# Feed-forward units in pairs by Strassen's seven products, in a two-layer decoder step on one core

## The chip, the core and the metric

One NeuronCore of a Trainium2 chip runs the whole program. The metric is the device time of one execution in microseconds (us), lower is better. Engines are named as in the profile: PE (TensorE, matmuls), PEld (its weight loads), DVE (VectorE), ACT (ScalarE), POOL (GpSimd), SP (SyncE, which issues most transfers).

## What is computed

A decoder trunk of two layers over 520 tokens (512 of a prompt, 8 of a sample group), model width 1024. Layer 0 mixes with retention and a spatial gating unit, layer 1 with a convolution module. After each mixer comes the feed-forward, which the change is about:

```python
x = x + y
f = rmsnorm(x, norm_ffn_g[l]) @ ffn_w1[l]          # 1024 -> 4096
x = x + jnp.square(jax.nn.relu(f)) @ ffn_w2[l]     # 4096 -> 1024
...
rmsnorm: x * rsqrt(mean(x * x) + 1e-6) * g
```

All data are float32.

## The kernel before

Activations lie in SBUF with features on the 128 partitions, in eight chunks `c` of 128 features by T = 520 tokens; tokens are taken in two halves of HALF = 260. A matmul takes a 128x128 piece of a weight (stationary) and 128x260 of activations (moving) and adds into a bank of PSUM. To keep float32 accuracy each operand is split into a high part in the type fp32r and the rest: ACT writes the high part (line 120 for weights), DVE subtracts it from the source (line 121, a tensor operation that reads two tiles in SBUF). Each product is made as high x high, high x low and low x high.

A "unit" (`unit`, `unit_mm`) makes 128 output features of all 520 tokens from 1024 input features. `load_w` fetches its weights (128 x 8 x 128, 512 KB, one transfer on SP's queue, three buffers `raw`), `split_half` splits four of the eight pieces at a time (five buffers each of `wh` and `wl`), and 8 x 3 x 2 = 48 matmuls follow, line 137. 

The feed-forward `ffn` takes the 4096 hidden features in four blocks `blk`. For a block, eight up units make 1024 hidden features: the result in PSUM is multiplied by the row of 1/rms `nm.r` and cut at zero by DVE (`ft`, line 671), squared and split by ACT (`fh`, line 673), POOL (`ff`, line 675) and DVE (`fl`, line 676). Then eight down units add the block's share to `x` (line 691). `Norm` holds `x * g` in split form (`hi`, `lo`), before the factor 1/rms; `finish` makes the row of 1/rms and is called in the middle of the first up unit. In the last block of layer 1, the last unit is made half by half and followed by the final norm and the output (`last_half`).

The other stages use the same helpers: projections of layer 0 (`in_units`), retention, the output projection (`opr` for the retention rows, `ops` for the gating rows), and in layer 1 `conv_in`, the taps (DVE, and ACT with POOL: line 798; some on PE by the diagonal tiles `diag`, line 726), and `conv_out`. A block between `ops` and the first feed-forward prepares the sample tokens' convolution from rows kept before (`hist`, line 703, on POOL).

Tiles come from pools. Each tag has a number of buffers, and an instruction that writes a tile waits for the last reader of the one that had the buffer. `big` has five buffers of 128 x 8 x 520; `mp` holds what the mixers need for the whole program; PSUM has two double banks `mm` and four single ones `auxA`, `auxB`. The order of the instructions on each engine is made ahead by a planner, from the program's order as priority and its own estimates of times. Each engine then runs its instructions strictly in that order.

Of the kernel before, what the change touches and what calls it, by code (L numbers as in the profile page):

```python
# [71 lines left out]
def trunk_kernel(tc, a, o):  # L72
    nc = tc.nc
    te, ve, se, pe_ = nc.tensor, nc.vector, nc.scalar, nc.gpsimd
    with ExitStack() as st:
# [4 lines left out]
        mp = st.enter_context(tc.tile_pool(name="mp", bufs=2))  # L80
        ps = st.enter_context(tc.tile_pool(name="ps", bufs=2, space=PSUM))
        dr = st.enter_context(tc.tile_pool(name="dr", bufs=1, space=DRAM))

# [25 lines left out]
        def load_w(ap, row, col):  # L109
            raw = wp.tile([P, C, P], F32, name="raw", tag="raw", bufs=3)  # L110
            nc.sync.dma_start(raw, ap[row:row + D, col:col + P].rearrange("(k p) n -> p k n", p=P))
            return raw
# [3 lines left out]
        def split_half(src, i):  # L116
            hi = wp.tile([P, KH, P], F32R, name="wh", tag="wh", bufs=5)
            lo = wp.tile([P, KH, P], F32R, name="wl", tag="wl", bufs=5)
            sp = src[:, i * KH:(i + 1) * KH, :]
            se.activation(hi, sp, AF.Copy)  # L120
            ve.tensor_sub(lo, sp, hi.bitcast(F32))  # L121
            return hi, lo

# [6 lines left out]
        def unit_mm(pts, w, x, mid=None):  # L130
            """pts (two halves of the tokens) = w^T x, three products of the split parts."""
            xh, xl = x
            for k in range(C):
                hi, lo = w[k // KH]
                for i, (wt, xt) in enumerate(((hi, xh), (hi, xl), (lo, xh))):
                    for hf in range(2):
                        te.matmul(pts[hf], wt[:, k % KH, :], xt[:, k, hf * HALF:(hf + 1) * HALF],  # L137
                                  start=k == 0 and i == 0, stop=k == C - 1 and i == 2)
                if mid and k == 4:
                    mid()  # L140

        def unit(pt, ap, row, col, x, mid=None):
            """pt = ap[row:row+1024, col:col+128]^T x."""
            unit_mm(halves(pt), split_w(load_w(ap, row, col)), x, mid=mid)
# [61 lines left out]
        def rsqrt_row(pts, e_col, eps, out, nxt=None):  # L206
            """out = (pts + eps) ** -0.5: ScalarE's estimate and one Newton step."""
# [16 lines left out]
        def row_mean(src, name):  # L224
            """mean over features of [P, T] partial sums, on every partition (two psum tiles)."""
# [7 lines left out]
        class Norm:  # L233
            """x * g split in two parts, and the row of 1/rms, chunk by chunk."""

            def __init__(self, g, name, final=False):
                self.g, self.name = g, name
                self.hi = None if final else bigt(name + "h", F32R)
                self.lo = None if final else bigt(name + "l", F32R)
                self.acc = tmp(name + "acc")  # L240
                self.y = None

            def chunk(self, c, xc, square=True):
# [7 lines left out]
                if square:  # L251
                    self.square(c, xc, ve if c >= C - 2 else pe_)

            def square(self, c, xc, eng):
                if c == 0:
                    se.activation(self.acc, xc, AF.Square)
                else:
                    sq = tmp(f"{self.name}sq")
                    se.activation(sq, xc, AF.Square)
                    if c == C - 2:  # L260
                        table(AF.Abs_reciprocal_sqrt, sq[:, :1])
                    eng.tensor_add(self.acc, self.acc, sq)

# [4 lines left out]
            def last_half(self, c, xc, hf, cols):  # L268
                """final norm of one half of the tokens, and the output."""
# [20 lines left out]
        W_IN = a["ab_w_in"]  # L290
        raw = wp.tile([P, C, P], F32, name="raw", tag="raw", bufs=3)
# [15 lines left out]
        for c in range(C):  # L307
            nm.square(c, x0[:, c, :], pe_)
# [654 lines left out]
```

## Time and profile before

| what | value |
|---|---|
| device time, median of 3 runs | 1362.54 us (1361.64 to 1364.06) |
| the profiled execution, from its first to its last instruction (span) | 1359.8 us |
| mean granted TensorE clock in it | 0.986 |
| busy: PE, DVE, ACT, POOL | 96%, 55%, 38%, 24% of the span |
| first feed-forward | 412.0 to 782.6 us of the span |
| second feed-forward | 975.1 to 1346.4 us |

The page gives the profiled execution's time as its span alone; the median of the runs is 2.7 us more. In a row of groups of instructions stand line, engine, operation, the tiles written and read, the sizes and the count, then the busy time in us and the mean of one in ns, then the idle time of the engine ahead of them and what ended it. A row of the chain gives a start and a duration in us, the engine, the tile written and the line: it is the work, followed back from the end, that each next piece waited for. A row of the timeline gives start, duration, engine, line and tiles, with the idle time before it in brackets. Rows of transfers give the queue, the count, KB each and the median time from issue to landing.

### The profile page before, as it was taken

Reading aid. Unit: us, or ns where it says so; the run is one execution under the profiler, and the core shown is the slowest. Engines: PE = TensorE matmul, PEld = TensorE weight load, DVE = VectorE, ACT = ScalarE, POOL = GpSimd, SP = SyncE. Lnnn points to the kernel's source line nnn. Section 1 sums busy time; section 2 is a strip of 40 time slices with the busy share of each in tenths; the row PEclk is TensorE's granted clock in tenths of the full one; section 3 lists DMA queues with packets and bytes.
Section 4 is the critical chain, followed back from the end, with each engine's and each line's share of the span. In section 5 each row is a group of like instructions: output and inputs, shape, how many; then the busy total and the mean of one; then the engine's idle time right before and its main releaser. Section 6 shows DMA issues by size and latency. Waiting matters only on the chain.

```text
span 1359.8 us, 26329 instructions
## 1 busy us (share of the span) xinstructions
PE 1312.0 (96%) x10946; PEld 1282.1 (94%) x10946; DVE 752.7 (55%) x1297; ACT 516.1 (38%) x868; POOL 326.2 (24%) x281
## 2 busy tenths in 40 slices
PE   7999999699999999999999999989999999999996
PEld 7999997699999999999999998958999999999996
DVE  7633668965646434334334589967853343443434
ACT  6433345323343223223223466647632232222342
POOL 4421013530011102002012149852220120110212
PEclk8999999899999999999999999999999999999998
DMA  7333247453332333333333332453533333333321
GB/s 242 95 93 105 82 132 254 143 172 93 94 94 79 94 94 94 94 94 94 90 87 91 90 86 71 141 134 105 160 94 94 94 93 90 89 89 93 94 78 64
DMA packets 242663, 145.04 MB, mean 107 GB/s; under 512 B 5984, under 2 KB 234336, under 8 KB 242544
## 3 DMA queue, kind: packets, MB, share of 16 engines
q1 hardware_dynamic: 239296, 134.11, 34.2%
q0 software_dynamic: 2304, 8.39, 1.7%
q8 instruction: 86, 1.41, 0.4%
q10 hardware_dynamic: 944, 0.86, 0.2%
q14 instruction: 33, 0.27, 0.1%
HBM read 135.15 MB, written 9.13 MB: 106 GB/s over the span
## 4 chain that ended last, share of the span: by engine, by line
PE 82%; DVE 11%; DMA 3%; issue 2%; ACT 1%; SPq 1%; DVEq 0%; ACTq 0%
PE f L137 27%; PE y L137 27%; PE in L137 13%; PE ops L137 3%; DVE cv L805 3%; PE opr L137 3%; PE co L154 2%; DVE wl L121 2%; DMA vb<-scr 2%; PE cvB L775 1%; PE ci L137 1%; DVE S L520 1%; PE opr L154 1%; DMA raw<-in_ab_w_out 0%; PE mx L644 0%
## 5 line engine op out<-in xcount | busy, mean ns | idle before, releaser
L120 ACT ACTIVATE wh<-raw 128x512 fp32r<-128x512 f32 x432 | 271.3, 630 | 656.3 <-PE y L137 250.4
L121 DVE TENSOR_TENSOR wl<-raw,wh 128x512 fp32r<-128x512 f32 x432 | 312.9, 726 | 205.4 <-ACT wh L120 204.2
L675 POOL TENSOR_TENSOR ff<-ft 128x520 f32<-128x520 f32 x64 | 86.9, 1358 | 575.7 <-DVE ft L671 554.8
L137 PE MATMUL y<-fh,wl 128*128 128x260 f32 x1008 | 203.1, 283 | 0.0
L137 PE MATMUL y<-fl,wh 128*128 128x260 f32 x1008 | 202.7, 283 | 0.0
L137 PE MATMUL y<-fh,wh 128*128 128x260 f32 x1008 | 201.5, 282 | 0.0
L137 PEld LDWEIGHTS y<-fh,wl 128*128 128x128 f32 x1008 | 155.3, 188 | 0.0
L137 PEld LDWEIGHTS y<-fl,wh 128*128 128x128 f32 x1008 | 155.0, 188 | 0.0
L137 PEld LDWEIGHTS y<-fh,wh 128*128 128x128 f32 x1008 | 154.8, 188 | 0.0
L137 PE MATMUL in<-n0h,wh 128*128 128x260 f32 x640 | 134.8, 291 | 5.9 <-ACT wh L120 5.9
L137 PE MATMUL in<-n0l,wh 128*128 128x260 f32 x640 | 132.9, 289 | 2.7 <-DVE n0l L246 2.4
L137 PE MATMUL in<-n0h,wl 128*128 128x260 f32 x640 | 132.3, 288 | 0.0
L137 PEld LDWEIGHTS in<-n0h,wh 128*128 128x128 f32 x640 | 101.2, 193 | 7.4 <-ACT wh L120 5.9
L691 DVE TENSOR_TENSOR x<-y,x 128x520 f32<-128x520 f32 x63 | 44.1, 700 | 115.0 <-PE y L137 115.0
L137 PEld LDWEIGHTS in<-n0l,wh 128*128 128x128 f32 x640 | 100.5, 192 | 4.8 <-DVE n0l L246 4.2
L137 PE MATMUL f<-n3h,wh 128*128 128x260 f32 x512 | 102.9, 282 | 0.6 <-DVE x L871 0.6
L137 PE MATMUL f<-n1h,wh 128*128 128x260 f32 x512 | 102.9, 282 | 0.5 <-DVE ft L671 0.5
L137 PE MATMUL f<-n3h,wl 128*128 128x260 f32 x512 | 103.4, 284 | 0.0
L137 PE MATMUL f<-n1l,wh 128*128 128x260 f32 x512 | 103.4, 283 | 0.0
L137 PE MATMUL f<-n1h,wl 128*128 128x260 f32 x512 | 103.2, 283 | 0.0
L137 PE MATMUL f<-n3l,wh 128*128 128x260 f32 x512 | 103.0, 283 | 0.0
L137 PEld LDWEIGHTS in<-n0h,wl 128*128 128x128 f32 x640 | 100.8, 192 | 1.4 <-issue 1.3
(335 smaller groups left out, 2381.5 us busy)
## 6 DMA issues: line engine op xcount, KB each, us to landing
raw<-in_ffn_w SPq DMA_DIRECT2D x128, 512.0 KB, 4.0
raw<-in_ab_w_in SPq DMA_DIRECT2D x39, 512.0 KB, 3.8
raw<-in_ab_w_out SPq DMA_DIRECT2D x16, 512.0 KB, 4.2
raw<-in_conv_w_in SPq DMA_DIRECT2D x16, 512.0 KB, 3.9
raw<-in_conv_w_out SPq DMA_DIRECT2D x16, 512.0 KB, 4.2
X<-xscr SPq DMA_DIRECT2D x32, 132.0 KB, 3.0
x<-in_xT SPq DMA_DIRECT2D x16, 260.0 KB, 4.8
S<-in_state_ret POOLq DMA_DIRECT2D x8, 512.0 KB, 5.5
```

Source lines behind the costliest of these rows:

```text
L120: se.activation(hi, sp, AF.Copy)
L121: ve.tensor_sub(lo, sp, hi.bitcast(F32))
L137: te.matmul(pts[hf], wt[:, k % KH, :], xt[:, k, hf * HALF:(hf + 1) * HALF], start=k == 0 and i == 0, stop=k == C - 1 and i == 2)
L154: te.matmul(pt, wt[:, k % KH, :], xt[:, k, cols], start=k == 0 and i == 0, stop=k == C - 1 and i == 2)
L520: ve.scalar_tensor_tensor(out=S0[:, h, :], in0=S0[:, h, :], scalar=float(GAMMA[h]), in1=vh, op0=ALU.mult, op1=ALU.add)
L675: pe_.tensor_mul(f, t, t)
L691: ve.tensor_tensor(h2(xc), ph2(pt), h2(xc), op=ALU.add)
L775: te.matmul(acc[32 * g:32 * g + 32, :], diag[c, k][:, g, :], X[:, g, k:k + HC], start=k == 0, stop=k == ns - 1)
L805: ve.scalar_tensor_tensor(out=o, in0=win(k), scalar=dw[:, c, k:k + 1], in1=acc, op0=ALU.mult, op1=ALU.add)
```

## The change

In the feed-forwards, units are taken in pairs i and KH + i (KH = 4). A pair's weights are four pieces of 512 x 128: a11, a12 of the first unit's inputs, a21, a22 of the second's, and the activations are cut into input chunks i and KH + i by token halves LO and HI. The 2 x 2 product of these blocks is made by seven products of half the inputs, half the outputs and half the tokens (Winograd's form of Strassen's scheme), each of 4 chunks x 3 parts = 12 matmuls of 128 x 128 by 260.

- `Pair.load` fetches both units' weights and has POOL make four sums of 512 elements per partition (`s1` to `s4`, tag `wsum`, four buffers). Each of the seven weight operands is split on ACT and DVE.
- `seven` makes the seven activation operands from four quarters of 260 tokens (`f4`): POOL three instructions into `t4`, ACT and DVE the split, three instructions each. It is used on the normed input (`norm_seven`, which also multiplies by g and 1/rms on DVE, three instructions) and on the hidden features (`hidden`).
- Banks: products 1, 6, 7, 4 of a pair go to one bank p on top of each other, 5 and 3 to q, 2 to r. `read` takes the partial sums out after each product: for up pairs by ACT (1, 6, 5, 4) and DVE (2, 3, 7), with the square made on DVE as max(f, 0) * f, or min for the sign-turned half; for down pairs by DVE into `x`.
- `run` puts a pair's product 4 behind products 1, 5, 2, 6 of the next pair (behind product 1 after the last up pair of a block). The first up pair of the next block is made before a block's down pairs. `run_behind` interleaves the first two down pairs of layer 0's last block.
- In block 0 the first PLAIN = 2 up pairs stay plain units; so do the down units of layer 1's last block, with their inputs in the order 0, 4, 1, 5, 2, 6, 3, 7.
- Memory: `mp` is opened anew for each stage (`open_stage`: mix0, ffn0, mix1, ffn1) over the same area, and waits go tile by tile. The feed-forward's tiles (`wide`, `f4`, `t4`, `f7`) and the norm's `hi` and `lo` lie in it. `raw` has four buffers for three, `wh` and `wl` four for five; the DMA scratch is set to 4096.
- Moved: the preparation from the kept rows goes ahead of the `ops` units; the copy out of the last tap rows (8 POOL copies, 2 transfers) goes ahead of `conv_out`. `diag` is made in the stage mix1, whose memory opens after the first feed-forward.

The diff, cut to its core:

```diff
+PLAIN = 2
+RAWS, SPLITS = 4, 4
...
+        def seven(f4, dst):
+            t4 = mp.tile([P, 4, HALF], F32, name="t4", tag="t4", bufs=1)
+            pe_.tensor_tensor(t4[:, 0:2], f4[:, 1:4:2], f4[:, 0:1].to_broadcast([P, 2, HALF]), op=ALU.subtract)
+            pe_.tensor_add(t4[:, 3], f4[:, 3], t4[:, 0])
+            pe_.tensor_sub(t4[:, 2], t4[:, 3], f4[:, 2])
+            for d, src in ((0, f4[:, 1:4]), (3, t4[:, 0:3])):
+                se.activation(dst[:, d:d + 3], src, AF.Copy)
+                ve.tensor_sub(dst[:, 7 + d:10 + d], src, dst[:, d:d + 3].bitcast(F32))
+            se.activation(dst[:, 6], t4[:, 3], AF.Copy, scale=-1.0)
+            ve.scalar_tensor_tensor(out=dst[:, 13], in0=t4[:, 3], scalar=-1.0, in1=dst[:, 6].bitcast(F32),
+                                    op0=ALU.mult, op1=ALU.subtract)
...
+            def load(self):
+                ap, row, cols = self.src
+                t, b = [load_w(ap, row, c) for c in cols]
+                a11, a12, a21, a22 = t[:, :KH], t[:, KH:], b[:, :KH], b[:, KH:]
+                s1, s2, s3, s4 = [wp.tile([P, KH, P], F32, name=f"S{i}", tag="wsum", bufs=4) for i in range(4)]
+                pe_.tensor_add(s1, a21, a22)
+                pe_.tensor_add(s2, s1, a11)
+                pe_.tensor_add(s4, s2, a12)
+                pe_.tensor_add(s3, a11, a21)
+                self.w = {1: a11, 2: a12, 3: s4, 4: a22, 5: s1, 6: s2, 7: s3}
...
+            def product(self, n, ks=range(KH)):
+                if n not in self.split:
+                    self.split[n] = split(self.w[n])
+                hi, lo = self.split[n]
+                bank = self.banks["r" if n == 2 else "q" if n in (5, 3) else "p"]
...
+                if ks[-1] == KH - 1:
+                    self.read(n, bank)
...
+        def run(pair):
+            pair.load()
+            pair.product(1)
+            if pending and pending[0].last:
+                flush()
+            pair.product(5)
+            pair.product(2)
+            pair.product(6)
+            flush()
+            pair.product(3)
+            pair.product(7)
+            pending.append(pair)
...
+            def up(blk, i):
+                if blk == 0 and i < PLAIN:
+                    up_plain(blk, i)
+                    return
+                f4 = four("f4")
+                def read(n, bank):
+                    if n in (1, 6, 5, 4):
+                        se.copy(f4[:, {1: 1, 6: 0, 5: 3, 4: 2}[n]], bank)
+                    else:
+                        c = f4[:, {2: 1, 3: 0, 7: 3}[n]]
+                        ve.tensor_tensor(c, bank, c, op=ALU.add)
+                    if n == 3:
+                        ve.scalar_tensor_tensor(out=f4[:, 0:2], in0=f4[:, 0:2], scalar=0.0, in1=f4[:, 0:2],
+                                                op0=ALU.max, op1=ALU.mult)
+                    if n == 4:
+                        ve.scalar_tensor_tensor(out=f4[:, 2:4], in0=f4[:, 2:4], scalar=0.0, in1=f4[:, 2:4],
+                                                op0=ALU.min, op1=ALU.mult)
+                        hidden(blk, i, f4)
...
+            for blk in range(4):
+                for i in range(1 if blk else 0, KH):
+                    up(blk, i)
+                if blk < 3:
+                    up(blk + 1, 0)
+                down(blk)
```

More of the change, by code (lines that the diff above doesn't have):

```diff
@@ L137, in unit_mm, with unit @@
                         te.matmul(pts[hf], wt[:, k % KH, :], xt[:, k, hf * HALF:(hf + 1) * HALF],
-                                  start=k == 0 and i == 0, stop=k == C - 1 and i == 2)
-                if mid and k == 4:
+                                  start=n == 0 and i == 0, stop=n == C - 1 and i == 2)
+                if mid and n == 4:
                     mid()
-        def unit(pt, ap, row, col, x, mid=None):
-            unit_mm(halves(pt), split_w(load_w(ap, row, col)), x, mid=mid)
+        def unit(pt, ap, row, col, x, mid=None, ks=range(C)):
+            unit_mm(halves(pt), split_w(load_w(ap, row, col)), x, mid=mid, ks=ks)
@@ new lines, in trunk_kernel, with __init__ @@
+        class Pair:
+            def __init__(self, ap, row, cols, x7, read, last=False):
+                self.src, self.x7, self.read, self.last = (ap, row, cols), x7, read, last
+            def load(self):
[8 more added lines that the diff above has]
+                self.w = {1: a11, 2: a12, 3: s4, 4: a22, 5: s1, 6: s2, 7: s3}
+                pq = mmt("pq")
+                self.banks = {"p": pq[:, 0, :HALF], "q": pq[:, 1, :HALF], "r": aux("pr")[:, :HALF]}
+                self.split = {}
+            def product(self, n, ks=range(KH)):
[3 more added lines that the diff above has]
+                bank = self.banks["r" if n == 2 else "q" if n in (5, 3) else "p"]
+                q = Q_OF[n]
+                for k in ks:
+                    xh, xl = self.x7[k][:, q], self.x7[k][:, 7 + q]
+                    for i, (wt, xt) in enumerate(((hi, xh), (hi, xl), (lo, xh))):
+                        te.matmul(bank, wt[:, k, :], xt, start=n in (1, 2, 5) and k == 0 and i == 0,
+                                  stop=i == 2, skip_group_check=True)
+                if ks[-1] == KH - 1:
+                    self.read(n, bank)
@@ new lines, in trunk_kernel, with flush, run_behind @@
+        pending = []
+        def flush():
+            while pending:
+                pending.pop().product(4)
+        def run(pair):
[10 more added lines that the diff above has]
+            pending.append(pair)
+        def run_behind(pairs):
+            early = range(KH - 1)
+            flush()
+            for p in pairs:
+                p.load()
+                for n in (1, 5, 2):
+                    p.product(n, early)
+            for p in pairs:
+                for n in (1, 5, 2):
+                    p.product(n, [KH - 1])
+                p.product(6)
+                if p is pairs[0]:
+                    p.product(3)
+                    p.product(7)
+            flush()
+            pairs[0].product(4)
+            pairs[1].product(3)
+            pairs[1].product(7)
+            pending.append(pairs[1])
@@ L290, in trunk_kernel @@
         W_IN = a["ab_w_in"]
-        raw = wp.tile([P, C, P], F32, name="raw", tag="raw", bufs=3)
+        raw = wp.tile([P, C, P], F32, name="raw", tag="raw", bufs=RAWS)
         nc.sync.dma_start(x0[:, 0, :], a["xT"][:, 0, :])
@@ L710, in trunk_kernel, with wide, four @@
         nc.sync.dma_start(o["conv_s"][:, :PAD - 1], a["hist"][:, 1:])
+        mp = open_stage("ffn0")
+        def wide(name, dt):
+            return mp.tile([P, C, T], dt, name=name, tag="wide", bufs=2)
+        def four(name):
+            return mp.tile([P, 4, HALF], F32, name=name, tag="f4", bufs=2)
+        nm = Norm(G_FFN0, "n1", at=wide)
+        for c in range(C):
+            pt = mmt(f"ops{c}")
+            unit(pt, a["ab_w_out"], D, c * P, (sguh, sgul))
+            xc = x[:, c, :]
+            ve.tensor_tensor(h2(xc), ph2(pt), h2(xc), op=ALU.add)
+            nm.chunk(c, xc)
@@ L900, in trunk_kernel @@
         nc.sync.dma_start(o["conv_s"][:, PAD - 1], hnew)
+        mp = open_stage("ffn1")
+        nm = Norm(G_FFN1, "n3", at=wide)
+        conv_out(0, nm)
+        conv_apply(1, rc)
+        conv_out(1, nm)
         nm4 = Norm(G_FIN, "n4", final=True)
         ffn(1, nm, nm4)
+        stage.close()
 def kernel(**inputs):
```

169 lines of the change are left out of this document (110 added, 59 removed).

## The prediction

> **What bounds the kernel now.** I read the page first (engine shares, then the chain that ended last), then the chain in order of time.
>
> ```profile
> PE 1312.0 (96%) x10946; PEld 1282.1 (94%) x10946; DVE 752.7 (55%) x1297; ACT 516.1 (38%) x868; POOL 326.2 (24%) x281
> PE 82%; DVE 11%; DMA 3%; issue 2%; ACT 1%; SPq 1%; DVEq 0%; ACTq 0%
> ```
> ```profile
> 412.00 7.56 PE f L137 x63
> 419.56 0.88 PE n1ms L229 x4
> ...
> 424.06 0.71 DVE ft L671
> 424.77 0.14 issue
> 424.91 34.84 PE f L137 x288
> 459.75 46.11 PE y L137 x384
> 505.86 46.13 PE f L137 x384
> ...
> 782.57 5.65 PE ci L137 x47
> ...
> 943.61 17.51 PE co L154 x144
> ...
> 975.07 6.46 PE f L137 x52
> ...
> 1339.33 4.32 PE yl L154 x36
> ...
> 1344.96 1.44 PE yl L154 x12
> ```
>
> Both feed-forwards (412.0 to 782.6, 975.1 to 1346.4) are matmuls without a break but for 3.6 us before 424.91: 384 in 46.12 us, 0.1201 each, and every 46.1 us block of eight units is the same. Nothing else is on the chain there. A unit is 48 matmuls, 5.77 us, so two units are 11.53. A stream into one bank at a time, as the products will be, keeps that pace (36 in 4.32; 144 in 17.51 with 264 columns for 260).
>
> **What comes off.** A pair becomes 7 x 4 x 3 = 84 matmuls in place of 96: 10.09 us, 1.44 less. Of 64 pairs, 2 up pairs per layer and the last block's 4 down pairs stay plain; 56 x 1.44 = 80.7 us leave TensorE.
>
> **What is added, per pair.** Rows of an up block of before:
>
> ```profile
> L121 DVE TENSOR_TENSOR wl<-raw,wh 128x512 fp32r<-128x512 f32 x16 | 11.0, 687 | 5.0 <-ACT wh L120 5.0
> L120 ACT ACTIVATE wh<-raw 128x512 fp32r<-128x512 f32 x17 | 10.7, 632 | 31.8 <-PE f L137 29.5 <-PE y L137 2.3
> L671 DVE SCALAR_TENSOR_TENSOR ft<-f,n1r 128x520 f32<-128x520 f32 x7 | 4.9, 700 | 12.0 <-PE f L137 12.0
> L676 DVE TENSOR_TENSOR fl<-ff,fh 128x520 fp32r<-128x520 f32 x7 | 4.9, 700 | 6.6 <-POOL ff L675 6.6
> ```
> ```profile
> L262 POOL TENSOR_TENSOR n1acc<-n1acc,n1sq 128x520 f32<-128x520 f32 x5 | 6.6, 1323 | 30.0 <-ACT n1sq L259 30.0
> L246 DVE SCALAR_TENSOR_TENSOR n1l<-x,par,n1h 128x520 fp32r<-128x520 f32 x8 | 6.1, 760 | 1.4 <-ACT n1h L245 1.4
> L686 DVE TENSOR_TENSOR x<-x,yl 128x260 f32<-128x260 f32 x2 | 0.9, 426 | 0.2
> L812 ACT COPY part<-cm 128x264 f32<-128x264 f32 x1 | 0.4, 381 | 0.9 <-PE cm L830 0.9
> ```
>
> Any pair: seven splits in place of four (ACT 7 x 0.632 = 4.4, DVE 7 x 0.687 = 4.8) and four weight sums on POOL (512 elements, about 1.3 each, 5.2). A down pair adds seven reads of a bank (0.43 each; before 2 x 0.70). An up pair adds four bank copies on ACT (0.38), three adds from a bank (0.43) and two 520-element squares (0.70) on DVE, and `seven`: POOL 520 + 260 + 260 elements (1.3 + 0.7 + 0.7, the shorter ones estimated from 1.32 at 520), ACT and DVE 780 + 780 + 260 each. By 0.43 at 260 and 0.70 at 520, 780 on DVE is 0.97. Sums of an up pair: DVE 4.8 + 1.3 + 1.4 + 2.4 = 9.9, POOL 7.9, ACT about 8.1. Each by itself lies under 10.09 and would be hidden. A down pair: DVE 7.8, POOL 5.2.
>
> **They are not by themselves.** Where DVE and POOL both read SBUF, this trace shows them taking turns:
>
> ```profile
> 7.03 11.75 POOL L262 TENSOR_TENSOR n0acc<-n0acc,n0sq 128x520 f32<-128x520 f32 x7 [6.12 <-ACT n0sq L259]
> 12.42 6.92 DVE L246 SCALAR_TENSOR_TENSOR n0l<-x,par,n0h 128x520 fp32r<-128x520 f32 x4
> ```
> ```profile
> 871.04 1.29 POOL L798 TENSOR_TENSOR pacc<-pacc,pp 128x512 f32<-128x512 f32 x1
> 871.43 1.46 DVE L121 TENSOR_TENSOR wl<-raw,wh 128x512 fp32r<-128x512 f32 x1
> 872.42 1.63 POOL L798 TENSOR_TENSOR pacc<-pacc,pp 128x512 f32<-128x512 f32 x1
> ```
> ```profile
> L121 DVE TENSOR_TENSOR wl<-raw,wh 128x512 fp32r<-128x512 f32 x28 | 29.8, 1065 | 0.0
> L750 DVE SCALAR_TENSOR_TENSOR xg<-ca,par,cg 128x512 f32<-128x512 f32 x6 | 7.0, 1166 | 0.0
> L798 POOL TENSOR_TENSOR pacc<-pacc,pp 128x512 f32<-128x512 f32 x54 | 80.3, 1494 | 4.3 <-ACT pp L797 1.7
> L807 POOL TENSOR_TENSOR cT<-cT,pacc 128x512 f32<-128x512 f32 x3 | 4.3, 1444 | 1.5 <-DVE cT L805 1.5
> ```
>
> Seven POOL adds take 1.68 each and four DVE operations 1.73 each in the same stretch, against 1.32 and 0.76 alone: one of each per 1.7 us. In the conv stage (800 to 890, the last four rows) a split that takes 0.687 alone takes 1.065. The three rows at 871 give the price of a turn: POOL ends at 872.33, DVE at 872.89 (0.56 later), POOL at 874.05 (1.16 later). So POOL holds the turn for 1.16 us per 512 elements (2.27 ns each), DVE for 0.55 (1.07 ns). DVE operations with one input in PSUM, as the bank reads are, take no turn: `ft` is 0.70 beside anything.
>
> Turns of an up pair: DVE 7 x 512 + 1040 + 1820 = 6444 elements, 6.9 us; POOL 2048 + 1040 = 3088, 7.0 us; 13.9 us against TensorE's 10.09 and the 11.53 of before. Of a down pair: 3584 elements, 3.8, and 2048, 4.7; 8.5 us, which TensorE covers. So up pairs become slower than before by 2.4 us and down pairs faster by 1.44.
>
> The Trainium skill, SBUF — State Buffer, Who interferes with whom, states this conflict for a VectorE instruction with two SBUF inputs and a GpSimd one that reads SBUF, and that the second to issue blocks until the first finishes.
>
> **The start of each feed-forward.** The row of 1/rms is there 12.1 us after the first matmul (424.06; taken for both layers). Four `norm_seven` follow: each DVE 1040 + 1820 elements and POOL 1040, 5.4 us of turns, 21.7 in all; with six splits of plain units (3.3) the seven operands stand at 37 us. The plain units cover 4 x 5.77 + 0.9 = 24. TensorE then waits some 13 us. The two plain pairs' `hidden` (5.4 each, 10.8) comes on top.
>
> **The sum, per layer.** Turns from 12.1 us on, up side: 21.7 + 3.3 + 10.8 + 14 x 13.9 = 230.4. Down side at TensorE's pace: 16 x 10.09 = 161.4 in layer 0, 12 x 10.09 + 46.1 = 167.2 in layer 1. POOL can make weight sums ahead while down pairs run: 1.6 us of idle turns per pair, 6.4 per block, at three boundaries at most 19, at least 0 as splits and reads also wait in order. I take 12, since raw, S and split buffers hold about a pair (6 of turns) ahead. Layer 0: 12.1 + 230.4 + 161.4 - 12 = 391.9 against 370.6, +21.3. Layer 1: 12.1 + 230.4 + 167.2 - 12 + 1.3 (last norm) = 399.0 against 371.3, +27.7. Together +49.
>
> Bounds: turns used 94% of the time as in the conv stage (57 x 1.16 + 34 x 0.55 = 84.8 of 90 us) adds 2 x 14.7 = 29. The full 19 ahead takes off 14. Whether the square `f4*f4`, which reads one tile twice, takes a turn, no row shows; if not, 32 x 1040 x 1.07 ns = 36 go. I count it, as the nearest rows (`n0l`) do with two inputs.
>
> **The smaller edits.**
>
> ```profile
> L137 PE MATMUL in<-n0h,wh 128*128 128x260 f32 x640 | 134.8, 291 | 5.9 <-ACT wh L120 5.9
> L726 POOL TENSOR_TENSOR diag<-ids,dws 128x1024 f32<-128x1024 f32 x4 | 8.4, 2106 | 6.0 <-DMA out_ret_s<-S 3.7 <-DVE rs_t L198 2.3
> L703 POOL TENSOR_TENSOR hist<-hist,dw 128x120 f32<-128x120 f32 x16 | 8.1, 542 | 47.8 <-DMA hist<-in_hist 47.8
> ```
> ```profile
> 797.39 0.21 POOL L898 COPY cst<-xg 128x30 f32<-128x30 f32 x1 [22.87 <-DVE xg L750]
> ```
> ```profile
> raw<-in_ffn_w SPq DMA_DIRECT2D x128, 512.0 KB, 4.0
> S<-in_state_ret POOLq DMA_DIRECT2D x8, 512.0 KB, 5.5
> hist<-in_hist SPq DMA_DIRECT2D x2, 480.0 KB, 7.5
> out_conv_s<-in_hist SPq DMA_DIRECT2D x1, 928.0 KB, 7.2
> ```
>
> Four split buffers for five, four raw for three: TensorE waited 5.9 us for splits in the projections; between 0 and as much again, less up to 3 for earlier loads; +1. `diag` (8.4 us of POOL) ran at 245 to 293 and can now run only when the conv stage opens, where POOL is the busiest; between the end of layer 0 (782.6) and its first work there (797.39) POOL idles 15 us, so 0, or 8 if it queues behind taps; +1. The kept rows (2 loads, the copy out, 16 POOL products, 4 DVE operations) move ahead of the gating projection's 8 loads on SP; those products ran there anyway (POOL waited 47.8 for the load) and raw buffers hold three units, 17 us, against 22 of transfers (2 x 7.5 + 7.2): 0, at most 5. The last tap rows' 8 copies and 2 transfers go past 16 loads of `conv_out`; they were ready before: 0. Opening a stage waits for the old tiles' readers, which end at or before the last unit: 0 to 2. A smaller DMA scratch could make the 16 state transfers wait for each other: 0, up to 8; 0. Loads are 1 MB per 10.1 us for 11.5: 4 us each, hidden. Together +2.
>
> The profiled span is 1359.8, 2.7 under the median of the runs shown. 1359.8 + 49 + 2 + 2.7 = 1413.5.
>
> **Rivals.** *TensorE keeps the pace (faster).* If turns overlap more than those rows show, each engine's own sum is under 10.09, and only the start is left: the operands come at 12.1 + 4 x 3.9 + 3 = 31 instead of 24, +7 per layer. 1362.5 - 80.7 + 14 = 1296. For it: the sums; against it: the 1.7 us per couple. It decides where the up-and-down turns, 22.4, fall under TensorE's 20.2, so with turns 10% cheaper.
> *Even.* The square takes no turn and POOL runs ahead by the full 19: 1413 - 36 - 14 = 1363; it is no change within 0.2%, about what a measurement of this kernel tells, in a narrow band only.
> *Queues add to the turns (slower).* Bank p is read after product 6 and written again two products, 2.9 us, later. If a read queued on DVE behind blocked splits loses one POOL operation (1.29) per up pair: 28 x 1.29 = 36, 1449.
> *The whole instruction is held.* A couple would then cost 1.32 + 0.70 = 2.02 rather than 1.70; the up side grows by 0.19 x 230 = 44 per layer, 1501. By the skill's page just named, read literally, it would be so; the trace does not agree, as DVE ends 0.56 after POOL, under its 0.687.
>
> **How the numbers follow.** Turns bind: 0.54, 1413, own range 1375 (square free, nothing else) to 1442. TensorE's pace: 0.18, 1280 to 1335. Even: 0.20, 1345 to 1372, of it 0.10 faster, 0.07 the same, 0.03 slower. Queues: 0.07; whole instruction: 0.01. Slower 0.54 + 0.03 + 0.08 = 0.65, same 0.07, faster 0.28. The range from 1312 to 1445 leaves out most of the second case and the last two.
>
> **What would show it.** Right: splits over 0.9 us and POOL adds over 1.5 in the up blocks; DVE and POOL busy over 90% there; up pairs at 13 to 15 us and down pairs near 10.1; a wait of some 13 us ahead of the first seven products; TensorE waiting for `wl`. Matmuls at 0.120 throughout. Wrong: splits near 0.69 beside POOL sums, or TensorE unbroken in up blocks.

## The result: 11% slower

| | before | after |
|---|---|---|
| device time, median (lowest to highest) | 1362.09 us (1360.44 to 1364.06) | 1506.93 us (1506.21 to 1508.07) |
| ratio, 95% interval | | 1.1063 [1.1048, 1.1079] |
| span of the profiled execution | 1359.8 us | 1505.0 us |
| mean granted TensorE clock | 0.986 | 0.948 |

The direction was right and the size was not: +145 us for a forecast of +51, and above the range's end of 1445.

From the page of after, engine shares, and the chain that ended last, by engine and by line:

```profile
PE 1308.8 (87%) x10274; PEld 1244.1 (83%) x10274; DVE 1196.6 (80%) x1781; ACT 682.1 (45%) x1204; POOL 735.5 (49%) x549
...
PE 59%; DVE 25%; issue 7%; ACT 3%; POOL 3%; DMA 2%; DVEq 0%; SPq 0%; ACTq 0%; POOLq 0%
PE pq L206 25%; PE in L148 13%; DVE wl L129 9%; PE pr L206 6%; PE ops L148 3%; DVE f L860 3%; PE y L148 3%; DVE cv L1012 2%; DVE f L172 2%; PE opr L148 2%; PE co L259 2%; POOL t L167 1%; ACT wh L128 1%; PE ci L148 1%; ACT f L171 1%
```

672 matmuls fewer are in the trace, as the change says, but TensorE's share fell from 96% to 87%, and DVE grew by 444 us and POOL by 409. DVE's weight splits (line 129) and squares (line 860) now stand on the chain, which before held nothing but matmuls there.

Stages of after, in windows: each row gives the stretch, its length, then busy time and count of PE, PEld, DVE, ACT and POOL, the granted clock, the DMA share and GB/s. In order: first feed-forward, conv stage, second feed-forward; then the first stretch of seven products, and the last down block of layer 0.

```profile
405.20:852.40 447.20, 367.33 (x2694) 348.14 (x2694) 395.69 (x491) 196.94 (x348) 273.93 (x184) 0.93 0.26 74
852.40:1057.10 204.70, 184.28 (x1716) 166.81 (x1715) 176.48 (x261) 126.24 (x223) 124.26 (x113) 0.96 0.41 112
1057.10:1491.60 434.50, 370.04 (x2770) 354.87 (x2770) 361.74 (x462) 192.91 (x346) 234.55 (x157) 0.93 0.26 74
431.02:492.25 61.23, 33.99 (x206) 31.09 (x204) 45.52 (x56) 23.81 (x43) 38.80 (x29) 0.72 0.15 43
800.88:852.40 51.52, 42.45 (x300) 39.69 (x300) 42.09 (x61) 24.90 (x42) 26.67 (x18) 0.93 0.26 73
```

The same first two stages of before:

```profile
411.80:782.50 370.70, 370.20 (x3079) 369.90 (x3078) 164.43 (x243) 112.61 (x180) 49.80 (x37) 1.00 0.32 92
782.50:975.00 192.50, 180.18 (x1693) 163.84 (x1691) 164.92 (x254) 122.80 (x217) 112.64 (x92) 0.97 0.41 115
```

| stage | before | forecast | after |
|---|---|---|---|
| up to the first feed-forward | 412.0 | +2 | 405.2 |
| feed-forward, layer 0 | 370.6 | 391.9 | 447.2 |
| conv stage | 192.5 | 192.5 | 204.7 |
| feed-forward, layer 1 | 371.3 | 399.0 | 434.5 |

DVE was busy 164 us of the first feed-forward before, 396 after. Inside it, one steady down block and one up block of after. 84 matmuls are a pair, and the pace of a pair is 84 x length / weight loads (the PEld count):

```profile
504.85:542.32 37.47, 34.35 (x278) 33.37 (x276) 35.15 (x47) 14.81 (x24) 23.93 (x17) 1.00 0.32 94
549.95:597.79 47.84, 38.43 (x265) 36.57 (x264) 43.33 (x47) 21.93 (x43) 31.66 (x22) 0.89 0.25 73
```

A down pair takes 11.40 us (forecast 10.1), an up pair 15.22 (forecast 13.9), where two plain units took 11.53. DVE is busy 94% and 91%. Its costliest groups in that up block, and POOL's:

```profile
L129 DVE TENSOR_TENSOR wl<-S,wh 128x512 fp32r<-128x512 f32 x13 | 13.7, 1068 | 1.4 <-ACT wh L128 1.4
L129 DVE TENSOR_TENSOR wl<-raw,wh 128x512 fp32r<-128x512 f32 x10 | 10.9, 1091 | 0.9 <-ACT wh L128 0.8
...
L860 DVE SCALAR_TENSOR_TENSOR f<-f 128x520 f32<-128x520 f32 x2 | 3.6, 1780 | 0.0
...
L855 DVE TENSOR_TENSOR f<-pq,f 128x260 f32<-128x260 f32 x6 | 2.5, 420 | 1.3 <-PE pq L206 1.3
```
```profile
L190 POOL TENSOR_TENSOR S<-S,raw 128x512 f32<-128x512 f32 x4 | 6.7, 1681 | 0.9 <-DVE wl L129 0.7
L191 POOL TENSOR_TENSOR S<-raw 128x512 f32<-128x512 f32 x4 | 6.7, 1664 | 0.0
...
L188 POOL TENSOR_TENSOR S<-raw 128x512 f32<-128x512 f32 x4 | 5.8, 1449 | 15.4 <-DMA raw<-in_ffn_w 8.4 <-DVE f L855 7.0
```

A split that took 0.687 us takes 1.07 to 1.09, POOL's adds reach 1.68 against 1.32 alone. The square of one tile (line 860, the same tile as both inputs) takes 1.78 here, and 0.70 in `sums_wait` below: it takes turns too, which the prediction had no row for. The pair's other square, line 857, is held less often (1.05 in this block). The bank reads (line 855) take 0.42 as ever. The last row shows POOL idle 15 us in the block ahead of its first sum, half of it for the load of the weights. In the down block the sums come in bursts; POOL's timeline (start, duration, tiles, idle before):

```profile
516.69 1.30 POOL L188 TENSOR_TENSOR S<-raw 128x512 f32<-128x512 f32 x1 [3.21 <-DVE wl L129]
518.07 1.63 POOL L189 TENSOR_TENSOR S<-S,raw 128x512 f32<-128x512 f32 x1
519.77 1.62 POOL L190 TENSOR_TENSOR S<-S,raw 128x512 f32<-128x512 f32 x1
521.35 1.74 POOL L191 TENSOR_TENSOR S<-raw 128x512 f32<-128x512 f32 x1
527.45 1.29 POOL L188 TENSOR_TENSOR S<-raw 128x512 f32<-128x512 f32 x1 [4.36 <-DVE x L871]
```

Four sums fill 6.4 us, one each 1.4 to 1.7 us with a split of DVE between them, and then POOL waits 4.4 us.

### The profile page after: what moved, and what is told of

Its sections match the earlier page's. It is cut to its first block, busy times and chain, and to the rows that moved or that the text cites. A ratio compares the mean times of both kernels' runs of the same rounds, so it can differ in the third digit from the quotient of the medians.

```text
span 1505.0 us, 26256 instructions
## 1 busy us (share of the span) xinstructions
PE 1308.8 (87%) x10274; PEld 1244.1 (83%) x10274; DVE 1196.6 (80%) x1781; ACT 682.1 (45%) x1204; POOL 735.5 (49%) x549
## 4 chain that ended last, share of the span: by engine, by line
PE 59%; DVE 25%; issue 7%; ACT 3%; POOL 3%; DMA 2%; DVEq 0%; SPq 0%; ACTq 0%; POOLq 0%
PE pq L206 25%; PE in L148 13%; DVE wl L129 9%; PE pr L206 6%; PE ops L148 3%; DVE f L860 3%; PE y L148 3%; DVE cv L1012 2%; DVE f L172 2%; PE opr L148 2%; PE co L259 2%; POOL t L167 1%; ACT wh L128 1%; PE ci L148 1%; ACT f L171 1%
## 5 line engine op out<-in xcount | busy, mean ns | idle before, releaser
L206 PE MATMUL pq<-x,wh 128*128 128x260 f32 x1344 | 271.5, 301 | 32.1 <-ACT f L852 12.1
L206 PE MATMUL pq<-f,wh 128*128 128x260 f32 x1344 | 258.8, 290 | 21.1 <-DVE f L172 9.6
L206 PEld LDWEIGHTS pq<-x,wh 128*128 128x128 f32 x1344 | 225.7, 205 | 39.4 <-ACT f L852 14.5
L129 DVE TENSOR_TENSOR wl<-S,wh 128x512 fp32r<-128x512 f32 x224 | 226.8, 1017 | 25.2 <-ACT wh L128 23.9
L206 PEld LDWEIGHTS pq<-f,wh 128*128 128x128 f32 x1344 | 210.9, 191 | 31.1 <-DVE f L172 11.5
L128 ACT ACTIVATE wh<-S 128x512 fp32r<-128x512 f32 x224 | 140.8, 630 | 197.2 <-PE pq L206 140.5
L206 PE MATMUL pq<-x,wl 128*128 128x260 f32 x672 | 202.3, 302 | 19.9 <-DVE wl L129 19.9
L206 PE MATMUL pq<-f,wl 128*128 128x260 f32 x672 | 194.0, 289 | 13.5 <-DVE wl L129 13.4
L188 POOL TENSOR_TENSOR S<-raw 128x512 f32<-128x512 f32 x56 | 80.3, 1434 | 231.7 <-DMA raw<-in_ffn_w 173.0
L189 POOL TENSOR_TENSOR S<-S,raw 128x512 f32<-128x512 f32 x56 | 88.9, 1587 | 23.3 <-issue 14.6
L191 POOL TENSOR_TENSOR S<-raw 128x512 f32<-128x512 f32 x56 | 95.3, 1702 | 1.3 <-DVE wl L129 1.3
L190 POOL TENSOR_TENSOR S<-S,raw 128x512 f32<-128x512 f32 x56 | 90.3, 1613 | 10.9 <-DVE wl L129 7.3
```

Of the source, the lines that this page charges most:

```text
L188: pe_.tensor_add(s1, a21, a22)
L189: pe_.tensor_add(s2, s1, a11)
L190: pe_.tensor_add(s4, s2, a12)
L191: pe_.tensor_add(s3, a11, a21)
L206: te.matmul(bank, wt[:, k, :], xt, start=n in (1, 2, 5) and k == 0 and i == 0, stop=i == 2, skip_group_check=True)
```

## The experiments

All are edits of the kernel after unless said otherwise. The planner lays out each kernel's order anew, so a few microseconds between two of them can be its doing.

**Whose work is it: the four weight sums.** `sums_dve` moves them to DVE:

```diff
-                pe_.tensor_add(s1, a21, a22)
+                ve.tensor_add(s1, a21, a22)
(and so s2, s4, s3)
```

> The four weight sums of a pair are made on DVE instead of POOL; all else is the changed kernel (1507). Theory of turns (DVE and POOL reading SBUF exclude each other): an up pair's turns fall from 13.9 to 9.1 + 2.4 = 11.5 us, a down pair's from 8.5 to 6.0; scaled by what the trace after shows against the ledger (15.3 for 13.9), up pairs come to about 12.6 and down pairs to 10.3: 28 x 2.7 + 28 x 1.1 = 107 less, about 1400. Rival, each engine is bound by its own list of work and DVE is the busy one: 4 x 0.6 us more per pair on DVE, 56 x 2.4 = 134 more, about 1640.

1467.36 us, ratio to before 1.0767 [1.0747, 1.0786]. Its down and up block:

```profile
501.31:540.40 39.09, 34.97 (x278) 33.55 (x276) 34.24 (x62) 14.80 (x24) 3.81 (x3) 1.00 0.33 94
547.80:587.62 39.82, 33.85 (x265) 32.05 (x264) 37.86 (x61) 22.23 (x43) 8.13 (x6) 1.00 0.30 86
```

2.8 us more of work a pair on the busiest engine made an up pair 2.5 us shorter (12.67): without POOL's sums DVE's other instructions run at their own lengths. But DVE stays 88 to 95% busy, and the down pairs go to 11.90. Both theories were off in size, turns by 67 us.

`no_sums` leaves the sums out (`s1, s2, s3, s4 = a21, a11, a21, a12`), `sums_set` puts three fills of the same tile in place of each:

```diff
+                for s in (s1, s2, s4, s3):
+                    for _ in range(3):
+                        pe_.memset(s, 0.001)
```

> The four weight sums are left out (products 5, 6, 3, 7 take raw pieces), so POOL has only the three sums of seven; DVE and ACT keep all their instructions. Turns: up pairs 6.9 + 2.4 = 9.3 us, under TensorE's 10.1, so near 10.3, down pairs 10.1: 28 x 5.0 + 28 x 1.3 = 176 less, about 1331, and splits near 0.69. Rival (DVE's and ACT's own queues, not POOL): nearly nothing comes off, 1480 to 1507.

> Each weight sum is replaced by three constant fills of the same tile on POOL, which write SBUF and read nothing; splits still wait for POOL. Turns, if it is the reading that excludes: as without sums, 1331 to 1345, splits near 0.69. If any POOL work or the wait for POOL's result is what costs: near the changed kernel, 1450 to 1507.

1399.57 and 1386.76 us (one run each). Blocks of `sums_set`:

```profile
581.03:615.21 34.18, 33.66 (x280) 33.40 (x278) 27.29 (x49) 15.34 (x25) 24.50 (x45) 1.00 0.37 106
534.87:571.11 36.24, 32.80 (x266) 31.75 (x264) 30.66 (x47) 22.00 (x43) 25.96 (x44) 1.00 0.32 92
```

POOL is busier than in after, 72% of both blocks for 64% and 66%, yet the pairs take 10.33 and 11.53. It is not POOL's work that costs, but what it does to SBUF, or its wait for the loads, since the fills read nothing and wait for no weights. Neither time came down to the expected 1331 to 1345: something else is left, some 40 to 70 us.

**Reads or loads.** Two kernels part these. `sums_wait` keeps the waits and all but removes the reads; `sums_own` keeps as many reads and removes the waits for the load. Both leave out the sums' values:

```diff
 sums_wait:
+                for s, i, j in ((s1, a21, a22), (s2, s1, a11), (s4, s2, a12), (s3, a11, a21)):
+                    for _ in range(2):
+                        pe_.memset(s, 0.001)
+                    pe_.tensor_add(s[:, :, :8], i[:, :, :8], j[:, :, :8])
 sums_own:
+                pe_.memset(s1, 0.001)
+                pe_.tensor_add(s1, s1, s1)
+                pe_.tensor_add(s2, s1, s1)
+                pe_.tensor_add(s4, s2, s1)
+                pe_.tensor_add(s3, s1, s2)
```

> The converse: each sum is two fills of its tile and an addition of 8 of 128 columns, so GpSimd's work and its waits for the loads stay as they are (about 1.3 us each) and its reads all but vanish; most of the values are left out. Theory A (reads): as with the fills alone, up 11.6, down 10.2, 1385 to 1400. Theory B (load buffers): up 14.5 to 15.3, down 11 to 11.5, 1480 to 1510. In between, both have a part, and the split of VectorE's wl (0.69 us bare, 1.0 now) says how much is turns.

> GpSimd fills the first sum tile and then does four additions of the same size, all of them on the sum tiles themselves: as many reads of SBUF as before, none of them behind the load of the weights; the values of the sums are left out. Theory A (GpSimd's reads set the pace by taking turns with VectorE): up pairs stay at 14.5 to 15.3 us, down pairs at 11 to 11.5, 1480 to 1510. Theory B (a loop of the four load buffers: the second tile of a pair is held until its last product is split in the next pair, so the load, then the burst of four sums, then the splits come late): with no wait for the load, pairs go to the 11.6 and 10.2 us of the fills, 1385 to 1410, although the reads stay.

1389.53 and 1464.42 us (one run each). Blocks (down, up) of `sums_wait`, its splits in the up block, and the blocks of `sums_own`, with the shortest of its other up blocks:

```profile
582.53:615.65 33.12, 33.12 (x278) 33.12 (x276) 26.70 (x47) 14.81 (x24) 21.35 (x46) 1.00 0.39 111
535.63:572.16 36.53, 32.82 (x266) 31.77 (x264) 30.93 (x47) 22.00 (x43) 25.34 (x45) 1.00 0.32 92
```
```profile
L129 DVE TENSOR_TENSOR wl<-S,wh 128x512 fp32r<-128x512 f32 x13 | 9.7, 749 | 2.2 <-ACT wh L128 2.1
L129 DVE TENSOR_TENSOR wl<-raw,wh 128x512 fp32r<-128x512 f32 x10 | 7.6, 762 | 2.4 <-ACT wh L128 2.2
```
```profile
595.54:634.47 38.93, 35.81 (x280) 35.05 (x278) 33.79 (x48) 15.33 (x25) 21.98 (x20) 0.96 0.33 94
541.25:584.82 43.57, 38.21 (x265) 36.30 (x264) 38.98 (x47) 21.94 (x43) 27.21 (x23) 0.88 0.28 79
1173.47:1214.40 40.93, 34.44 (x266) 32.27 (x265) 39.92 (x47) 22.08 (x43) 25.66 (x22) 1.00 0.29 85
```

With the same waits and no reads to speak of, the down block runs without a break (33.12 of 33.12 us, 10.08 a pair) and the splits are back at 0.75: the reads of the sums are worth 117 of the 145 us. With the reads and no waits for loads, up pairs take 13.86 in the first block and 12.97 in the shortest, about the 13.9 of the counted turns (two of these sums read one tile twice and take 1.04 us, so they count for less). Down pairs take 11.76, where turns fill only 8.5. So the wait for the loads costs time as well, up to 42 us of the 145, but only where the sums read (without reads it is 1389.5 with the waits and 1386.8 without): the two shares overlap and do not add up. The part of the reads fits the Trainium skill, SBUF — State Buffer, Who interferes with whom, which has the conflict with a GpSimd instruction that reads SBUF and not with one that only writes it.

`set_all` takes POOL's other reads in the pairs away too: fills as in `sums_set`, and two fills for each of the three differences `t4`, those of `norm_seven` at the start included.

> GpSimd reads nothing of the on-chip memory in the pairs: the four weight sums are three fills each of the same tiles, and the three differences of a hidden pair are two fills each; the values of both are left out. Theory (only GpSimd's reads hold VectorE up, and in the up pairs the differences' reads are what is left after the fills of the sums at 1386.8): up pairs go from 11.6 us to 10.1 to 10.5, the start loses some 10 us less a layer because no operand waits for GpSimd's arithmetic; 1310 to 1345. Rival (the up pairs' 11.6 us is VectorE's own work, 10.6 us busy, with its uneven arrival): up pairs stay at 11.3 to 11.6 and the time at 1365 to 1387.

1327.91 us (one run). Blocks:

```profile
558.18:591.22 33.04, 33.04 (x277) 33.04 (x276) 25.62 (x47) 14.81 (x24) 20.66 (x40) 1.00 0.36 103
514.24:548.92 34.68, 32.68 (x266) 31.80 (x264) 28.69 (x49) 22.52 (x45) 26.68 (x63) 1.00 0.34 97
```

Up pairs went to 11.03 only, and the first feed-forward lasts 349 us to the first matmul of the conv stage, 21 less than before the change. The scheme's gain is there as soon as POOL reads nothing, 34 us under before; the full 80.7 are not, even then.

**What makes 15.2 of 13.9, and 11.4 of 8.5.** `few_reads`: DVE's ten additions from PSUM touch 8 columns each.

```diff
-                    ve.tensor_tensor(x[:, c, cols], x[:, c, cols], bank, op=op)
+                    few = slice(cols.start, cols.start + 8)
+                    ve.tensor_tensor(x[:, c, few], x[:, c, few], bank[:, :8], op=op)
...
-                        ve.tensor_tensor(c, bank, c, op=ALU.add)
+                        ve.tensor_tensor(c[:, :8], bank[:, :8], c[:, :8], op=ALU.add)
```

> VectorE's ten additions from a PSUM bank (three of an up pair, seven of a down pair, 0.42 us each at 260 columns) touch 8 columns each; the rest of the sums is left out. Everything that takes turns with GpSimd is unchanged. Theory (a pair's pace is the turns plus VectorE's own reads of PSUM, since VectorE is one queue in order: 13.9 + 1.3 = 15.2 and 8.5 + 2.9 = 11.4): up pairs go to about 14.2, down pairs to TensorE's 10.1 to 10.5; 28 x 1.1 + 28 x 1.1 = 60 to 75 us less: 1430 to 1450. Rival (the turns alone set the pace, the reads fit in beside GpSimd's turns): up 15, down 11.4, 1495 to 1507.

1500.05 us, ratio 1.1008 [1.0941, 1.1076]. The theory that turns and PSUM reads add up is refuted: up pairs stay at 15.19, the down pairs of the block shown go to 12.33 instead of down to 10.1, and DVE waits instead. The reads are shorter here, but they still stand in DVE's one queue.

```profile
502.26:542.77 40.51, 34.95 (x277) 33.48 (x276) 33.03 (x46) 14.47 (x24) 25.92 (x18) 1.00 0.30 86
550.55:598.29 47.74, 38.55 (x265) 36.46 (x264) 41.09 (x47) 22.11 (x43) 31.59 (x22) 0.89 0.25 70
```

`split_early` frees the load buffer sooner, by splitting the held back product's weights at the end of their own pair; `split_up` does so in the up pairs alone.

```diff
             pair.product(7)
+            pair.split[4] = split(pair.w[4])
             pending.append(pair)
```

> The split of the held back product's weights (a22) is made at the end of its own pair instead of in the middle of the next one, which sets the second load buffer free some 6 us sooner and holds one of the four split buffers longer. Theory B (load buffers): the load comes sooner, pairs lose about 1 us: 1440 to 1475. Theory A (reads): nothing gained, a split buffer fewer for the products ahead: 1500 to 1530.

> The early split of a22 in the up pairs alone; the down pairs keep the late one. Theory (in the up pairs the wait for a load buffer costs what turns do not: they went from 15.2 to 13.4 us in split_early): 28 x 1.8 = 50 less, 1455 to 1470. Rival (the early split only moves the wait to the change between up and down pairs, where the held split buffer is missing): 1490 to 1515.

1551.69 us, 1.1382 [1.1333, 1.1431], and 1507.61 us, 1.1069 [1.1049, 1.1088]. Down and up block of `split_early`, then an up block of `split_up`:

```profile
505.26:553.91 48.65, 39.89 (x277) 38.93 (x276) 36.17 (x48) 14.80 (x24) 21.96 (x18) 0.86 0.23 67
562.64:604.79 42.15, 34.15 (x266) 32.10 (x264) 40.42 (x47) 21.59 (x43) 26.82 (x19) 1.00 0.26 76
```
```profile
548.74:593.89 45.15, 35.63 (x265) 33.62 (x264) 41.09 (x47) 21.88 (x43) 30.00 (x21) 0.96 0.28 79
```

Up pairs take 13.41 and 14.37, but the down pairs of the first go to 14.81, and in the second the whole kernel gains nothing; where it loses the gain of the up blocks again was not followed block by block. Its time is in the range of its rival, but that rival's cause, a wait at the changes between up and down pairs, was not shown. In the up pairs a wait for loads is the likely cause of a good part of the 1.3 us beyond the turns, since these go in `sums_own`. For the down pairs the part beyond the turns stays open.

**The start.** `start_two` gives each `norm_seven` an `xn` and `t4` of its own in the two `f7` buffers, free at that time. `start_dve` makes the three differences of `norm_seven` on DVE. `plain_four` has PLAIN = 4. `keep_clock` adds 200 matmuls into an unused bank after the plain units.

```diff
 start_two:
-                xn = four("xn")
+                room = mp.tile([P, 14, HALF], F32, name="room", tag="f7", bufs=2)
+                xn, t4 = room[:, :4], room[:, 4:8]
...
-                seven(xn, t)
+                seven(xn, t, t4)
 start_dve:
-                seven(xn, t)
+                seven(xn, t, ve)
 keep_clock:
+                if i == PLAIN - 1:
+                    idle = aux("idle")[:, :HALF]
+                    for n in range(200):
+                        te.matmul(idle, nm.hi[:, n % C, :P], nm.hi[:, n % C, :HALF], start=n == 0, stop=n == 199)
```

> The changed kernel with the four norm_seven at each start working in the two f7 buffers (free at that time), so that xn and t4 have two buffers of their own in place of one t4 between all. Theory that the one t4 makes the four a chain: the operands stand about 11 us sooner (the 37 us of the ledger for the 48 seen), 20 to 28 us less in all, about 1483. Theory that turns alone set it: the turns are the same, 1500 to 1507.

> Only the four operand builders of each layer's start compute their three differences on VectorE instead of GpSimd. Theory (VectorE and GpSimd wait for one another in turn, about 13 us for an operand of which VectorE works 5): an operand takes some 6 us, the fourth is ready about 24 us after the norm's factors instead of 36, and 10 to 15 us a layer come back: 1477 to 1487. Rival (the splits of the weights decide the start, the operands are late because VectorE is full): VectorE gets 1.4 us more work for each operand, time 1503 to 1515.

> Four pairs of the first up block in the plain form instead of two; eight plain units take 8 x 5.77 = 46 us and the operands of the seven products, complete 48 us after the start of the feed-forward part, are ready when they are first wanted. Theory (TensorE stands at the start because the operands are late): the 36 us lost at the start of each layer shrink to under 10, two more plain pairs cost 2.9, so 2 x (26 - 3) = about -45: 1455 to 1470. Rival (VectorE bounds the start by the sum of its work, so the loss only moves): the operands are as late against the work as before, or VectorE's backlog is paid in the next block; 1490 to 1510.

> The changed kernel with 200 matmuls without use (24 us, into a spare bank) behind the two plain pairs of each layer, where TensorE waited some 28 us and the granted clock then read 0.50 to 0.75 until 470. If the clock costs time: it stays at 1.0, some 130 matmuls that ran at half pace come back, 6 to 8 us per layer, about 1493. If the waits hide it: 1505 to 1510.

1505.17, 1503.31 (1.1035 [1.1015, 1.1055]), 1495.77 (1.0971 [1.0951, 1.099]) and 1510.33 us. None gives back much more than 11 us for two layers: the first theory of each fell. In after the fourth operand's last VectorE step starts at 452.3, 47 us after the feed-forward's start; with the differences on DVE it starts at 448.7, and from the factors of the norm on DVE is full (busy 31.58 of 31.80 us):

```profile
417.80:449.60 31.80, 17.95 (x119) 15.99 (x118) 31.58 (x55) 12.76 (x19) 3.39 (x3) 0.79 0.12 34
```

There the sum of DVE's work sets the start. In after it does not, as 30 us of it show, with the same stretch of `set_all` below:

```profile
430.00:460.00 30.00, 8.63 (x37) 6.71 (x37) 21.00 (x29) 9.70 (x15) 22.65 (x16) 0.60 0.06 18
430.00:460.00 30.00, 23.66 (x173) 22.41 (x174) 25.70 (x44) 18.27 (x35) 21.50 (x53) 0.94 0.24 71
```

DVE is busy 21 of 30 us in after. Where POOL's differences read nothing and wait for nothing of DVE, TensorE loads 174 weights in that stretch and not 37. `sums_wait`, which keeps the differences, loads 44. So POOL's differences hold the start of after, by their reads or because the operands wait for their results; no run parts the two. On DVE they gain next to nothing, as DVE is then full. Why four plain pairs gave 11 us and not 45 was not followed. The granted clock in the gap, after and then `keep_clock`:

```profile
443.00:455.00 12.00, 4.36 (x15) 3.46 (x15) 9.29 (x14) 4.62 (x7) 7.88 (x7) 0.50 0.00 0
```
```profile
443.00:455.00 12.00, 12.00 (x102) 12.00 (x101) 7.94 (x13) 3.76 (x6) 6.46 (x6) 1.00 0.00 0
```

The clock fell to 0.50 where TensorE stood; holding it up gained nothing, and the operands came no sooner (the fourth's last step starts at 452.5).

**Parts of the change alone.** `plain_newmem` has the feed-forward of before in plain units and everything else of the change. `down_pool` takes only the down pairs by seven products (up pairs by `up_plain`, followed by `flush()`; `f7` and the last block's `fh`, `fl` in `big`), `down_dve` the same with the sums on DVE, `down_wait` is `down_pool` with the sums of `sums_wait`.

> Feed-forward units as in the kernel before, in the new memory with everything else of the change (stages, four raw and four split buffers, moved blocks, smaller scratch). In the trace after, the part ahead of the first feed-forward is 6.8 us shorter and the conv stage 12.2 longer. If the 12.2 belong to memory and moved work (the diagonal tiles on POOL): 1362 - 7 + 12 = 1367. If they are the pairs' work left over at the end of layer 0: 1355.

> Only the down pairs are made by seven products, with the weight sums on DVE; all up units are plain. Turns: a down pair has 6.0 us on DVE and none on POOL, DVE's own work 9.0 to 9.5, so 10.1 to 10.4 per pair; the up pairs have 7.6 us of turns under TensorE's 11.53. From the kernel with plain units in the new memory (1355): 28 x 1.2 to 1.4 less, 1316 to 1321. Rival, waits at the changes between up and down (the seventh operand, reads of banks) eat it: 1335 to 1355.

> The same with the weight sums on POOL. Turns 8.5 us per down pair: if only their sum matters, hidden, as with DVE (1316 to 1321). If the burst of four sums alternating with splits sets the pace, as the rows of the changed kernel suggest (10.7 to 11.4 per pair): 1332 to 1351.

> Down pairs alone by seven products, with the sums as fills and an addition of 8 columns (most of their values are left out), to be set against down_pool at 1370.8. Theory (the 50 us that down_pool lacks against its count are GpSimd's reads, in the down blocks 11.1 to 11.5 us a pair, and in the last block of the first layer 15): down pairs go to 10.1 to 10.3, 1310 to 1335. Rival (the change between plain units and pairs, or the norm's work in the last block, takes the gain): 1350 to 1370.

| | us | ratio to before |
|---|---|---|
| `plain_newmem` | 1354.61 | 0.9944 [0.9931, 0.9958] |
| `down_dve` | 1381.85 | 1.013 [1.0099, 1.016] |
| `down_pool` | 1370.8 | 1.0054 [1.0038, 1.007] |
| `down_wait` | 1343.91 (one run) | |

The first two stages of interest of `plain_newmem`, feed-forward and conv stage:

```profile
404.70:775.90 371.20, 370.27 (x3080) 369.77 (x3079) 162.61 (x239) 112.36 (x180) 59.51 (x57) 1.00 0.32 92
775.90:967.90 192.00, 178.77 (x1693) 162.15 (x1692) 165.59 (x254) 123.27 (x217) 111.30 (x92) 0.97 0.42 115
```

The memory and the moved steps gain 7 us ahead of the first feed-forward and cost nothing later; the conv stage's 12 us belong to the pairs. `plain_newmem`, at 0.994 of before, is the fastest kernel here that computes everything. An up block, a down block, and layer 0's last down block of `down_pool`:

```profile
516.35:556.85 40.50, 40.50 (x340) 40.50 (x339) 33.52 (x43) 15.66 (x26) 18.91 (x14) 1.00 0.28 83
556.69:597.70 41.01, 38.31 (x314) 37.64 (x313) 37.25 (x55) 16.45 (x26) 22.52 (x15) 1.00 0.32 91
725.32:780.80 55.48, 46.07 (x315) 44.06 (x314) 44.96 (x64) 24.52 (x41) 27.16 (x19) 0.88 0.24 68
```

The plain up block is without a break, but the down pairs take 11.0, and 14.8 where the norm of the conv stage joins them. Taking the reads away (`down_wait`) gives 27 us, of the 50 that the count lacks: its time lies between the two theories' ranges. Here are a down block and the conv stage of `down_wait`, then a down block of `down_dve`:

```profile
553.92:593.19 39.27, 37.96 (x315) 37.58 (x314) 31.01 (x54) 16.46 (x26) 21.89 (x44) 1.00 0.33 93
762.10:969.30 207.20, 186.73 (x1718) 168.85 (x1716) 177.20 (x262) 127.01 (x223) 124.86 (x113) 0.95 0.40 111
```
```profile
557.01:600.41 43.40, 39.37 (x315) 37.94 (x313) 36.73 (x65) 16.43 (x26) 3.42 (x3) 1.00 0.30 86
```

The largest part of what `down_wait` still lacks (28 x 1.44 off `plain_newmem` would be 1314) is in the conv stage: 207.2 us for 192.0, although POOL's sums read next to nothing. Its steady down pairs take 10.5. `down_dve` missed both its ranges: without any sum on POOL its down pairs take 11.65, with DVE busy 9.9 of them. An engine's list under TensorE's 10.1 is thus no cover here, even without turns with POOL's sums.

## Why the prediction was right in sign and wrong in size

**Right.** The matmuls' pace: a down block without reads runs 276 of them in 33.12 us, 0.120 each. Turns as the mechanism that binds: splits over 0.9, POOL's adds over 1.5 (the first of a pair 1.45), DVE over 90% in the up blocks; and without the reads of the sums, at the same waits, 1506.9 becomes 1389.5. Turns also make 13.0 to 13.9 an up pair in `sums_own`, for 13.9 counted at most. The square takes a turn. One more sign failed: POOL, foretold at over 90% in the up blocks, is busy 66%. Of the rivals, TensorE's pace and the even case did not come; the whole instruction being held (1501) gives nearly the time but not the rows: the sums of a burst follow each other every 1.4 to 1.7 us with a split between them, and 1.32 + 0.69 would be 2.0. "Queues add to the turns" (1449) has by its 1.29 an up pair the size of point 2 below. Its mechanism, a read queued on DVE behind blocked splits, was not tested: `few_reads` shortens the reads and leaves them in the queue, and 7.0 of POOL's 15.4 idle us in the up block follow such a read (line 855).

**Wrong, step by step,** with what each is worth in the 94 us by which the forecast was short:

1. *Of a down pair "8.5 us, which TensorE covers".* It does not: 11.40 against 10.09, 28 x 1.31 = 37 us, and layer 0's last down block takes 51.52 us for 300 matmuls, 14.4 a pair, some 11 more. In `sums_wait` it is 10.08, so POOL's reads do it, although the turns would fit. The step compared sums over a pair, and that is no cover: see `down_dve`. The trace shows a burst, one sum and one split per 1.4 to 1.7 us where TensorE uses a split each 1.44, and idle turns after it. That the burst is the reason is not shown, and one run speaks against it as the whole: in `sums_own` the sums come one by one (for one pair at 603.6, 606.0, 609.1 and 611.0), and its down pairs take 11.76. How the reads stretch a down pair to 11.40 stays open.
2. *Up pairs 13.9.* 15.22: 28 x 1.3 = 37 us. Turns were taken to be filled without a gap; POOL idles 15 us in an up block of 48, more than half of it for a load. Where no sum waits for a load (`sums_own`, one run), up pairs come to 13.0 to 13.9, so that wait is a good part of the step (some 0.5 us of the difference can be its two shorter sums); PSUM reads by their length are not it (`few_reads`), and freeing the load buffer sooner gained nothing in all (`split_up`). The bound of the prediction for this ("turns used 94%", +29) was nearly enough by itself.
3. *The credit of 12 us a layer* for sums made ahead. From 492.25 to 852.40 layer 0 has 972 matmuls of up and 1320 of down pairs; at the paces above, with the 11 us of the last block, they are 366.1 us and took 360.2, so 5.9 came: 6 a layer short, 12 in all if layer 1 is the same.
4. *Nothing in the conv stage.* +12, and 9 beyond what the forecast has elsewhere: two products of the last pair (24 matmuls, 2.9 us, counted in the feed-forward) run behind the first matmuls of the conv stage. The matmuls of that stage's norm start 15.3 us behind its first matmul, in `plain_newmem` 5.65; the last pair's reads of `x` come ahead of it. Turns with POOL are not the reason: `set_all` has 205.9 us there, `down_wait` 207.2, `plain_newmem` 192.0.
5. *The smaller edits, +2.* They gain: the stretch to the first feed-forward is 6.8 shorter, about 9 us the other way. Which edit does it was not tried.
6. *The start.* In sum it was nearly right: the count has 47.9 us of turns and then pairs, so 204 matmuls done 47.9 + 2.43 x 13.9 = 81.7 us after the start; they were done at 87.1 (492.25). 3.2 of the 5.4 are point 2, 2 a layer are left. That was partly luck, as the operands stood 48 us after the start for the 37 counted. The wait was laid out wrongly too: the 13 us, and the plain pairs' 10.8 "on top", are one wait of TensorE, busy 8.6 of the 30 us from 430 to 460, while DVE makes the operands and the plain pairs' `hidden` by turns.

37 + 11 + 37 + 12 + 9 - 9 + 4 is 101, for 94 measured; layer 1 was not counted out row by row, and 7 us are not assigned.

The largest single error is the first: the down pairs were booked as the change's gain of 1.44 each, and gained 0.1.

## What to carry to other kernels

An algorithm that saves matmuls pays in elementwise work. Where VectorE reads two SBUF tiles and GpSimd reads SBUF as well, add the two engines' times up, and do not take a pair's total below TensorE's as cover: look at the order in which the work arrives. To tell a port's conflict from an engine's load or a wait, replace the second engine's work with fills of about the same length and the same waits: a few lines, and here 117 of the 145 us were attributed. Then keep the reads and take the waits away, since the two can overlap.

## What the chip showed that was not expected

- POOL's fills beside DVE's two-input operations: twelve of 0.5 us a pair, POOL 72% busy, splits at 0.76 to 0.83 in the up block of `sums_set`, where POOL's differences still read, and 0.70 to 0.73 in the down block (bare 0.69). Only with the sums' reads did the splits go to 1.07 and more.
- DVE with one operation after the other can hold POOL off for longer than one turn each. On the chain of after, at the start:

```profile
430.09 3.75 POOL t L167
```

  This 520-element difference takes 1.3 us alone; it began while DVE ran five two-input operations in a row at their bare lengths, from 429.1 to 432.7, and ended 1.1 us behind the last of them.
- The granted clock fell to 0.50 in a gap of TensorE and cost nothing that could be measured, where what the gap waits for is not on TensorE (`keep_clock`, 1510.3). The Trainium skill, TensorE: Matmul & The Clock Gate, Part 1, has the same half step for an idle TensorE; the rows agree.
